# Hybrid decoder block on one core: three sums of w_down's quarters made by adding transfers in DRAM, and MLP activations kept as float32 sums

## The chip, the cores and the metric

The kernel runs on one core of one Trainium2 chip, as one launch. The metric is the device time in microseconds. Engines: TensorE (PE, with PEld for its weight loads), VectorE (DVE), ScalarE (ACT), GpSimd (POOL) and SyncE (SP, which only issues transfers). 16 DMA engines move data for all queues.

## What is computed

One decoder block over 512 tokens of width 1024. Attention has a sparse mixer and a recurrent mixer, merged and projected; then comes a gated MLP of width 2816 with a causal convolution of width 3, and a residual. Only the MLP's end matters here:

```python
def conv_ffn(h, w_up, conv_w, conv_b, w_down):
    u = h @ w_up
    ...
    val, gate = jnp.split(c, 2, axis=-1)          # c: the convolution of u
    return (jax.nn.silu(gate) * val) @ w_down     # (512 x 2816) @ (2816 x 1024)
```

## The kernel before

**Precision.** Every float32 operand of a projection is split into two float32r halves, high and low: ACT copies the high half (`whi`), DVE or POOL subtracts it from the value (`wlo`). A product is then three passes of matmuls: high by high, low by high, high by low.

**Seven products for eight.** The down projection is cut in quarters: the activations in tokens 0 to 255 and 256 to 511, and features 0 to 1407 (left: `l0`, `l1`) and 1408 to 2815 (right: `r0`, `r1`); w_down in the same halves of rows, and halves of columns. Seven products of sums of quarters replace eight products of quarters. They are called by number. The activations' factors are `l0` (1), `s1 = l1 + r1` (5), `s2 = s1 - l0` (6), `s3 = l0 - l1` (7), `s4 = r0 - s2` (3), `r0` (2) and `r1` (4). The weights' factors are the first quarter (1), the difference of two quarters (5), that of three (6), a difference (7), a quarter (3), another (2), and a difference of all four (4). Each product runs over `CH`, six blocks of 256 rows of weights (one of 128). The list `items` has 42 entries, in three groups: for each block products 1, 5, 6; then for each block 7, 3; then 2, 4. In PSUM, products 1 and 2 use the banks `BX` (`ps_a`), 5 and 3 `BY` (`ps_b`), 6, 7 and 4 `BZ` (`ps_mm`). At the end of product 6 and of product 5 DVE adds earlier results (`ev`, kept by ACT) into a bank, and products 7 and 3 go on in it.

**Who prepares.** In the MLP, `sums` makes for each pair of feature tiles the four sums on DVE, and splits `l0`, `s1`, `s2`, `s3` at once (`split`, four ACT copies and four DVE subtractions of 128x256). In the down projection, `prepare` runs two items ahead of `product`: it calls `difference` (a subtraction of weights on DVE: the sums for 5, 6, 7 and 4), splits the weights (`parts`) and, for products 3 and 4, the activations (`operand`). `spare_half` splits the right half's `r0` into the place of `l0` two items after each item of product 1. `load_next` issues the loads of w_down on SP into six places, each when its last user is prepared. Here PE, DVE and ACT run in the order of the program.

**Attention.** PE's order is the program's; a loop over twelve `units` makes scores, transposes and values, and puts matmuls of two projections between them (`filler`). From 298 us these are the eight tiles of w_proj_b, each eight matmuls with `whi` and then four with `wlo`. The subtraction for `wlo` of these eight tiles is made by POOL (line 307), in its queue among its transfers.

Of the kernel before, what the change touches and what calls it, by code (L numbers as in the profile page):

```python
# [12 lines left out]
F32 = mybir.dt.float32  # L13
F32R = mybir.dt.float32r
# [69 lines left out]
def hybrid_block(ctx: ExitStack, tc: tile.TileContext, A: dict, out: bass.AP):  # L84
# [203 lines left out]
    urgent = []  # L288

    def wsplit_():  # L290
        if loads:
# [1023 lines left out]
    nfill = [5, 5, 6, 6, 7, 8, 10, 10, 10, 9, 9, 6]  # L1315
    with tc.manual_schedule(engines=KTS):
# [4 lines left out]
        for i, u in enumerate(units):  # L1321
            if u not in quarters:
                turns(u)
# [136 lines left out]
    tmp = hB[:, 256 * NFH:256 * (NFH + 3)].rearrange("p (k n) -> p k n", k=3)  # L1460
    split = [fp.tile([128, 2, NFH, 256], F32R, name=f"s{j}", tag=f"s{j}") for j in range(4)]
# [20 lines left out]
    w_down = A["w_down"][0]  # L1482
# [8 lines left out]
    for js, last, froms in (((1, 5, 6), (1, 6, 5), ((1, 0, 0), (5, 0, 1), (6, 1, 1))),  # L1491
                            ((7, 3), (7, 3), ((7, 0, 1), (3, 1, 1))), ((2, 4), (2, 4), ((2, 1, 0),))):
        for c, n in CH:
            items += [(j, c, n) for j in (last if c + n == NFH else js)]
            at = {q[0]: k for k, q in enumerate(items) if q[1] == c}
            last_of = {1: (1, 5), 5: (5, 6), 6: (0, 6), 7: (7, 7), 3: (3, 7), 2: (2, 4)}
            fetch += [(*f, c, n, tuple(at[q] if q else 0 for q in last_of[f[0]])) for f in froms]

    raws, turns3, turn, place, start, users = {}, itertools.count(), places(), [], [], [(-1, -1)] * 6

    def load_next():
# [3 lines left out]
        i = place[0]  # L1505
        if not fetch or len(ready) <= users[i][0] or len(summed) <= users[i][1] or (i > 3 and not T2):
            return False
        j, kh, fh, c, n, users[i] = fetch.pop(0)
# [6 lines left out]
        r0 = 128 * (NFH * kh + c)  # L1515
        nc.sync.dma_start(raw, w_down[r0:r0 + 128 * n, 512 * fh:512 * fh + 512].rearrange("(k p) n -> p k n", p=128))
        raws[j, c] = raw
        return True

    def parts(x, n):  # L1520
# [3 lines left out]
        else:  # L1524
            hi, lo = (dn.tile([128, 1024 + p_], F32R, name=k, tag=k)[:, 0:512 * n].rearrange("p (k n) -> p k n", k=n)
# [5 lines left out]
    summed = []  # L1531
# [20 lines left out]
    T1 = set()  # L1552
# [7 lines left out]

    def operand(j, c, n):
# [9 lines left out]
    ready, T2, Sb, X1 = [], [], [], []  # L1571

    def prepare():
        k = len(ready)
        j, c, n = items[k]
        while len(summed) < min(k + 2, len(items)):
            difference()
        ready.append((parts(summed[k], n), operand(j, c, n)))
# [6 lines left out]
    for n_, f in enumerate(order):  # L1585
# [9 lines left out]
        if n_ % 2 == 0:  # L1595
            tt(cv, cv, cg, ALU.mult)
            left = cv
# [4 lines left out]
    dn_cm, dn = pool("down", "right")  # L1602
    T2.append(dn.tile([128, NFH, 512], F32, name="T2"))
# [4 lines left out]
    def add_out(t, hf, x, cs=slice(0, 512), queue=None):  # L1608
        o = X1[0][:, hf, t, cs]
        tt(o, o, x, ALU.add)  # L1610
# [102 lines left out]
```

## Time and profile before

| | us |
|---|---|
| median of three runs (813.38 to 814.07) | 813.43 |
| profiled execution | 813.09 |
| its span | 811.4 |
| PE busy | 801.7 |
| DVE busy | 589.8 |
| ACT busy | 428.8 |
| POOL busy | 66.1 |

The span is what the profiler saw of one execution; 1.7 us of its time lie around it. A busy time counts the time in which an engine has an instruction in work. PE's matmuls overlap, so the pace is read from the distance of starts. Issuing a transfer is not counted as busy, save on POOL, where the row of an issue is its time on that engine. The MLP's up projection runs from about 450 to 701 us, the down projection from 701 to 807.

### The profile page before, as it was taken

The page shows a single profiled execution, that of the slowest core. Times are in us where ns is not written, and L with a number is a line of the kernel's source. Part 1 is how long each engine was busy: PE and PEld are TensorE (multiplying, and loading weights), DVE is VectorE, ACT ScalarE, POOL GpSimd, SP SyncE. Part 2 cuts the span into 40 slices and gives each one's busy share as a digit, 9 for nine tenths or more (in the row PEclk, how much of TensorE's full clock was granted, in tenths as well). Part 3 has the DMA queues.
Part 4 walks back from the last instruction along what each step waited for, and adds up shares of the span by engine and source line. Part 5 has one row for each costly group of instructions (what it writes and reads, how often), then busy time and mean ns, then how long its engine had stood idle before and what let it go on. Part 6 is the DMA issues. An engine that isn't in the chain of part 4 may idle for free.

```text
span 811.4 us, 13524 instructions
## 1 busy us (share of the span) xinstructions
PE 801.7 (99%) x5253; PEld 654.7 (81%) x5253; DVE 589.8 (73%) x1139; ACT 428.8 (53%) x851; POOL 66.1 (8%) x98
## 2 busy tenths in 40 slices
PE   8999999999999999999999999999999999999997
PEld 7777788987777887787888988888888888887886
DVE  6478879983656678889665576677667666898895
ACT  6766654553545668778344454444444444446452
POOL 6100011031000152111000000000000000000010
PEclk9999999999999999999999999999999999999999
DMA  8422223237471331000268133332333233467721
GB/s 242 111 78 76 78 70 87 70 97 216 114 131 53 92 81 28 27 27 27 67 228 277 66 91 92 105 104 84 99 103 102 82 104 104 127 224 231 261 92 52
DMA packets 114124, 89.26 MB, mean 110 GB/s; under 512 B 4629, under 2 KB 98764, under 8 KB 113804
## 3 DMA queue, kind: packets, MB, share of 16 engines
q1 hardware_dynamic: 110416, 82.31, 34.3%
q0 software_dynamic: 2592, 3.61, 1.7%
q10 hardware_dynamic: 1052, 2.48, 1.0%
q8 instruction: 41, 0.67, 0.3%
q14 instruction: 23, 0.19, 0.1%
HBM read 82.35 MB, written 4.39 MB: 107 GB/s over the span
## 4 chain that ended last, share of the span: by engine, by line
PE 94%; DVE 3%; ACT 1%; DMA 1%; issue 1%; POOL 0%; DVEq 0%; POOLq 0%; ACTq 0%
PE ps_mm L123 72%; PE ps_a L123 7%; PE ps_b L123 4%; PE ps_mm L126 3%; PE ps_b L126 2%; PE ps_a L126 2%; PE ps_b L1288 1%; DMA pra<-in_rwkv_ln_b_dram 1%; PE ps_mm L1288 1%; DVE P L1214 0%; POOL pra L170 0%; DVE P L136 0%; ACT P L129 0%; ACT whi L129 0%; PE ps_b L575 0%
## 5 line engine op out<-in xcount | busy, mean ns | idle before, releaser
L123 PE MATMUL ps_mm<-hh,whi 128*128 128x512 f32 (+1 forms) x624 | 242.5, 391 | 0.3 <-DVE hl L141 0.3
L123 PE MATMUL ps_mm<-hl,whi 128*128 128x512 f32 (+1 forms) x624 | 240.3, 387 | 0.0
L129 ACT ACTIVATE whi<-raw 128x1024 fp32r<-128x1024 f32 (+3 forms) x118 | 116.3, 987 | 118.3 <-PE ps_mm L123 87.2
L307 DVE TENSOR_TENSOR wlo<-raw,whi 128x1024 fp32r<-128x1024 f32 (+1 forms) x89 | 104.4, 1174 | 90.1 <-PE ps_mm L123 69.4
L123 PE MATMUL ps_mm<-hh,wlo 128*128 128x512 f32 (+1 forms) x624 | 152.1, 384 | 0.0
L123 PEld LDWEIGHTS ps_mm<-hh,whi 128*128 128x128 f32 x624 | 117.2, 188 | 27.0 <-issue 1.3
L123 PEld LDWEIGHTS ps_mm<-hl,whi 128*128 128x128 f32 x624 | 117.3, 188 | 23.0 <-issue 1.0
L123 PEld LDWEIGHTS ps_mm<-hh,wlo 128*128 128x128 f32 x624 | 115.1, 188 | 23.5
L141 DVE SCALAR_TENSOR_TENSOR hA<-ps_mm,cw,hA 128x511 f32<-128x511 f32 (+1 forms) x88 | 65.4, 746 | 1.5
L129 ACT ACTIVATE hA<-ps_mm,cw 128x512 f32<-128x512 f32 x44 | 34.2, 781 | 19.9 <-PE ps_mm L123 18.3
L129 ACT ACTIVATE P<-P,nm 128x512 f32<-128x512 f32 (+3 forms) x64 | 35.4, 554 | 11.3 <-DVE nm L1214 10.9
L1612 POOL DMA_DIRECT2D out_dram<-XP x6 | 3.3, 546 | 422.3 <-DMA raw<-in_w_down_dram 396.3
L129 ACT ACTIVATE hA<-hA 128x512 f32<-128x512 f32 x22 | 13.9, 633 | 43.6 <-DVE hA L141 43.6
L307 POOL TENSOR_TENSOR wlo<-raw,whi 128x512 fp32r<-128x512 f32 (+3 forms) x13 | 20.9, 1605 | 176.8 <-PE ps_mm L123 142.5
L1214 DVE CUSTOM_DVE_ANT_0 P<-ps_a,AB 128x512 f32<-128x512 f32 (+3 forms) x64 | 29.3, 484 | 1.8 <-PE ps_a L123 1.5
L129 ACT ACTIVATE QK<-ps_mm 128x64 f32<-128x64 f32 (+5 forms) x56 | 14.9, 308 | 18.0 <-PE ps_mm L123 17.9
L132 DVE TENSOR_TENSOR wlo<-raw,whi 128x1024 fp32r<-128x1024 f32 (+1 forms) x16 | 18.5, 1155 | 5.5 <-ACT whi L129 5.5
L123 PE MATMUL ps_mm<-whi,hh 128*128 128x280 f32 (+2 forms) x72 | 22.4, 331 | 0.0
L123 PE MATMUL ps_mm<-whi,hl 128*128 128x280 f32 (+2 forms) x72 | 21.8, 323 | 0.0
L123 PE MATMUL ps_mm<-obT,whi 128*128 128x512 f32 x64 | 20.7, 399 | 0.0
L129 ACT ACTIVATE whi<-T 128x1024 fp32r<-128x1024 f32 (+1 forms) x12 | 11.9, 991 | 16.4 <-DVE T L132 7.5
L129 ACT ACTIVATE whi<-hA 128x1024 fp32r<-128x1024 f32 (+1 forms) x14 | 13.4, 969 | 12.8 <-PE ps_mm L126 3.7
(436 smaller groups left out, 1507.4 us busy)
## 6 DMA issues: line engine op xcount, KB each, us to landing
raw<-in_w_up_dram SPq DMA_DIRECT2D x44, 512.0 KB, 3.7
raw<-in_w_in_dram SPq DMA_DIRECT2D x38, 512.0 KB, 3.8
raw<-in_w_down_dram SPq DMA_DIRECT2D x18, 512.0 KB, 4.1
hA<-in_w_down_dram SPq DMA_DIRECT2D x12, 512.0 KB, 4.6
raw<-in_w_out_dram SPq DMA_DIRECT2D x8, 512.0 KB, 3.6
xt<-in_x_dram SPq DMA_DIRECT2D x4, 512.0 KB, 4.6
raw<-in_cmp_w_v_dram SPq DMA_DIRECT2D x4, 512.0 KB, 3.6
raw<-in_w_proj_b_dram SPq DMA_DIRECT2D x8, 256.0 KB, 2.6
```

What stands on the lines that cost most here:

```text
L123: te.matmul(o, lhsT=l, rhs=r, start=start, stop=stop)
L126: te.matmul(o, lhsT=l, rhs=r, start=False, stop=stop, skip_group_check=True)
L129: sc.activation(o, i, f, **kw)
L132: v.tensor_tensor(o, a, b, op=op)
L141: v.scalar_tensor_tensor(o, a, s, b, op0=op0, op1=op1)
L307: low = eng.tensor_tensor(lo, raw, hi.bitcast(F32), op=ALU.subtract)
L1214: maxima.append(v.tensor_tensor_reduce(out=P[:, i], in0=o, in1=BT[:, h, 384 - 128 * qt:512], scale=-1.0, scalar=-NEG, op0=ALU.add, op1=ALU ...
L1288: te.transpose(pt[:, 128 * i:128 * i + 128], P[:, 4 * x + i, 128 * k:128 * k + 128], ident)
L1612: queue.dma_start(out[0][128 * t:128 * t + 128, 512 * hf + cs.start:512 * hf + cs.stop], o)
```

## The change

Three tensors in DRAM, `T1`, `T2`, `T3` (1408 x 512 each), receive sums of quarters of w_down. POOL issues six transfers from DRAM to DRAM in attention: three copies at unit 1, two that add to what is there at unit 7, and one at unit 11. The signs of the activations are chosen so that the weights are only added: `T1` is the sum of two quarters, `T3` of two others, `T2` of three. Product 4's sum (`T2` plus a quarter) is still made on DVE. Each of the 42 items now has a load of its own.

In the MLP, `sums` makes four float32 sums and splits nothing. In the down projection `operand` splits the activations of products 1, 5, 6, 7 and 3 into three buffers in turn (`Sb`), and `spare_half` splits both parts of the right half for products 2 and 4 (`pre`). Two stores of the output move from POOL's queue to SP's.

```diff
+    w_down = A["w_down"][0]
+    WD = [[w_down[DFF // 2 * i:DFF // 2 * (i + 1), 512 * j:512 * j + 512] for j in range(2)] for i in range(2)]
+    T1, T2, T3 = (dp.tile([DFF // 2, 512], F32, name=f"td{j}") for j in range(3))
+
+    def moved(o, x, **kw):
+        d = nc.gpsimd.dma_start(o, x, max_dma_last_dim=1024, **kw)
+        after(d, on_pool[0])
+        on_pool[:] = [d]
+
+    def weight_sums(i):
+        if i == 1:
+            moved(T1, WD[0][0])
+            moved(T3, WD[0][1])
+            moved(T2, WD[1][1])
+        elif i == 7:
+            moved(T1, WD[0][1], accum_op=ALU.add)
+            moved(T3, WD[1][1], accum_op=ALU.add)
+        elif i == 11:
+            moved(T2, T1, accum_op=ALU.add)
...
         for i, u in enumerate(units):
+            weight_sums(i)
...
-    def sums(i, lf, rt):
-        l0, l1, r0, r1 = lf[:, 0:256], lf[:, 256:512], rt[:, 0:256], rt[:, 256:512]
-        s1, s2, s3 = (tmp[:, j] for j in range(3))
-        tt(s3, l0, l1, ALU.subtract)
-        tt(s1, l1, r1, ALU.add)
-        tt(s2, s1, l0, ALU.subtract)
-        tt(s4[:, i], r0, s2, ALU.subtract)
-        for w, x in zip(split, (l0, s1, s2, s3)):
-            act(w[:, 0, i], x)
-            tt(w[:, 1, i], x, w[:, 0, i].bitcast(F32), ALU.subtract)
+    def sums(i, l1, rt):
+        tt(s3[:, i], a1[:, i], l1, ALU.subtract)
+        tt(s1[:, i], rt[:, 256:512], l1, ALU.subtract)
+        tt(s2[:, i], s1[:, i], a1[:, i], ALU.add)
+        tt(s4[:, i], s2[:, i], rt[:, 0:256], ALU.subtract)
...
+    source = {1: WD[0][0], 5: T1, 6: T2, 7: T3, 3: WD[1][1], 2: WD[1][0], 4: T2}
...
+        nc.sync.dma_start(raw, source[j][128 * c:128 * (c + n)].rearrange("(k p) n -> p k n", p=128))
...
     def difference():
-        j, c, n = items[len(summed)]
-        x = raws.get((j, c))
-        if j == 1 and items[len(summed) + 1][0] == 6 or j == 5 and (5, c) not in T1:
-            T1.add((5, c))
-            y = raws[5, c]
-            tt(y, y, raws[1, c], ALU.subtract)
-        if j == 6:
-            t = T2[0][:, c:c + n]
-            tt(t, x, raws[5, c], ALU.subtract)
-            x = t
-        elif j == 7:
-            tt(x, raws[3, c], x, ALU.subtract)
-        elif j == 4:
-            t = T2[0][:, c:c + n]
-            tt(t, raws[2, c], t, ALU.subtract)
-            x = t
-        summed.append(x)
+        k = summed[0]
+        if items[k][0] == 4:
+            tt(raws[k], raws[k], raws[k - 1], ALU.add)
+        summed[0] += 1
...
     def operand(j, c, n):
-        if j in (1, 5, 6, 7):
-            w = split[(1, 5, 6, 7).index(j)]
-            return w[:, 0, c:c + n], w[:, 1, c:c + n]
-        if j == 2:
-            return split[0][:, 0, c:c + n], split[0][:, 1, c:c + n]
-        x = s4[:, c:c + n] if j == 3 else right[:, c:c + n, 256:512]
-        i = next(turnsb) % 5
-        return halves_of(*(Sb[0][:, i, q, 0:256 * n].rearrange("p (k n) -> p k n", k=n) for q in range(2)), x)
+        if j in (2, 4):
+            return pre[0][:, j // 4, 0, c:c + n], pre[0][:, j // 4, 1, c:c + n]
+        x = {1: a1, 5: s1, 6: s2, 7: s3, 3: s4}[j][:, c:c + n]
+        i = next(turnsb) % 3
+        return halves_of(*(Sb[:, i, q, 0:256 * n].rearrange("p (k n) -> p k n", k=n) for q in range(2)), x)
...
     def spare_half(c, n):
-        halves_of(split[0][:, 0, c:c + n], split[0][:, 1, c:c + n], right[:, c:c + n, 0:256])
+        for q in range(2):
+            halves_of(pre[0][:, q, 0, c:c + n], pre[0][:, q, 1, c:c + n], right[:, c:c + n, 256 * q:256 * q + 256])
...
-                if j == 1:
+                if j == 1 and c < CH[-1][0]:
                     spare_half(c, n)
+                elif j == 3 and c == CH[0][0]:
+                    spare_half(*CH[-1])
```

On POOL the transfers of attention stand among the splits of w_proj_b (`wlo`); `td_3314`, `td_3316` and `td_3315` are `T1`, `T3` and `T2`. Before:

```order
L1105 DMA sq<-kc 32x64 x6
L307 TENSOR_TENSOR wlo<-raw,whi 128x512
L1103 DMA Vr<-vt 32x256 x16
L1105 DMA sq<-kc 32x64 x2
L307 TENSOR_TENSOR wlo<-raw,whi 128x512 x7
L1612 DMA out_dram<-XP 128x512 x6
```

And in the changed kernel:

```order
L1105 DMA Vr<-vt 32x256 x16
L1107 DMA sq<-kc 32x64 x2
L307 TENSOR_TENSOR wlo<-raw,whi 128x512
L1324 DMA td_3314<-in_w_down_dram 1408x2x256
L1324 DMA td_3316<-in_w_down_dram 1408x2x256
L1324 DMA td_3315<-in_w_down_dram 1408x2x256
L307 TENSOR_TENSOR wlo<-raw,whi 128x512 x3
L1324 DMA td_3314<-in_w_down_dram 1408x2x256
L1324 DMA td_3316<-in_w_down_dram 1408x2x256
L307 TENSOR_TENSOR wlo<-raw,whi 128x512 x3
L1324 DMA td_3315<-td_3314 2816x256
L1617 DMA out_dram<-XP 128x512 x4
```

Three issues stand ahead of the third tile's split, two ahead of the sixth's, one behind the last.

On DVE, where product 6 and then product 5 end (the additions into `ps_mm` and `ps_b`), `hA<-hA` and `raw<-hA,raw` being subtractions of weights and `s_5187` the place of the spare half. Before:

```order
L132 TENSOR_TENSOR wlo<-raw,whi 128x1024
L132 TENSOR_TENSOR ps_mm<-ps_mm,hA 128x512 x2
L132 TENSOR_TENSOR hA<-hA 128x1024
L132 TENSOR_TENSOR wlo<-hA,whi 128x1024
L132 TENSOR_TENSOR Sb<-hB,Sb 128x512
L132 TENSOR_TENSOR s_5187<-right,s_5187 128x512
L132 TENSOR_TENSOR ps_b<-ps_b,hA 128x512 x2
```

And in the changed kernel:

```order
L132 TENSOR_TENSOR wlo<-raw,whi 128x1024
L132 TENSOR_TENSOR Sb<-s_5198,Sb 128x512
L132 TENSOR_TENSOR ps_mm<-hA,ps_mm 128x512 x2
L132 TENSOR_TENSOR wlo<-hA,whi 128x1024
L132 TENSOR_TENSOR Sb<-hB,Sb 128x512
L132 TENSOR_TENSOR ps_b<-ps_b,hA 128x512 x2
```

Between the two additions two operations are gone, a subtraction of weights and the spare half's split.

On DVE at the MLP's end, from the last convolution on (line 141), with the splits of the second and third product's weights (`wlo`, `wlo_6833` and `wlo_6763`). Before:

```order
L132 TENSOR_TENSOR T_6812<-raw 128x1024
L141 SCALAR_TENSOR_TENSOR hA<-ps_mm,cw,hA 128x511
L132 TENSOR_TENSOR wlo<-raw,whi 128x1024
L141 SCALAR_TENSOR_TENSOR hA<-ps_mm,cw,hA 128x510
L132 TENSOR_TENSOR wlo_6833<-T_6812,whi_6832 128x1024
L132 TENSOR_TENSOR right<-hA 128x512
L132 TENSOR_TENSOR raw<-raw,hA 128x1024
```

And in the changed kernel, where the second product's weight split is the operation ahead of the first row:

```order
L141 SCALAR_TENSOR_TENSOR hA<-ps_mm,cw,hA 128x511
L132 TENSOR_TENSOR Sb<-a1s_5196,Sb 128x512
L141 SCALAR_TENSOR_TENSOR hA<-ps_mm,cw,hA 128x510
L132 TENSOR_TENSOR wlo_6763<-raw,whi_6762 128x1024
L132 TENSOR_TENSOR right<-hA 128x512
L132 TENSOR_TENSOR Sb<-s_5197,Sb 128x512
L132 TENSOR_TENSOR a1s_5196<-right,hA 128x256
```

The weight subtractions (`T_6812`, `raw<-raw,hA`) are gone, and splits of activations (`Sb`) stand between.

## Rows read from the trace of the kernel before

**Rows 1.** The page's busy time, share of the span and instructions by engine

```profile
PE 801.7 (99%) x5253; PEld 654.7 (81%) x5253; DVE 589.8 (73%) x1139; ACT 428.8 (53%) x851; POOL 66.1 (8%) x98
```

**Rows 2.** Waits of PE, whole span: us in total, times, longest

```profile
PE ps_b L126 <- DVE ps_b L132: 0.7, 1, 0.7
```

**Rows 3.** Stretches: length; busy PE, PEld, DVE, ACT, POOL; clock; DMA share; GB/s

```profile
0.00:50.00 50.00, 46.49 (x221) 36.68 (x221) 31.93 (x72) 32.24 (x48) 17.36 (x31) 1.00 0.57 164
350.00:400.00 50.00, 49.21 (x575) 38.97 (x575) 39.93 (x154) 32.62 (x108) 4.32 (x4) 1.00 0.13 39
...
740.00:750.00 10.00, 9.35 (x42) 7.43 (x40) 8.54 (x12) 7.39 (x11) 0.00 (x0) 1.00 0.69 227
800.00:811.40 11.40, 6.92 (x37) 5.78 (x35) 5.68 (x9) 1.49 (x2) 1.08 (x2) 0.94 0.25 93
```

**Rows 4.** Chain that ended last, down projection: start, us, engine, line, count

```profile
709.08 2.72 PE ps_a L123 x12
711.80 2.96 PE ps_b L123 x12
```

**Rows 5.** Timeline of ACT and DVE, product 5's end: start, us, what, idle before

```profile
745.25 1.05 ACT L129 ACTIVATE whi<-hA 128x1024 fp32r<-128x1024 f32 x1
746.34 1.23 DVE L132 TENSOR_TENSOR wlo<-hA,whi 128x1024 fp32r<-128x1024 f32 x1 [0.55 <-ACT whi L129]
...
748.08 0.68 DVE L132 TENSOR_TENSOR s<-right,s 128x512 fp32r<-128x512 f32 x1
748.68 1.29 DVE L132 TENSOR_TENSOR ps_b<-ps_b,hA 128x512 f32<-128x512 f32 x2
```

**Rows 6.** Timeline of DVE and PE at the MLP's end

```profile
700.96 1.23 DVE L132 TENSOR_TENSOR T<-raw 128x1024 f32<-128x1024 f32 x1 [2.52 <-PE ps_mm L123]
...
702.10 0.74 DVE L141 SCALAR_TENSOR_TENSOR hA<-ps_mm,cw,hA 128x511 f32<-128x511 f32 x1
...
702.76 1.22 DVE L132 TENSOR_TENSOR wlo<-raw,whi 128x1024 fp32r<-128x1024 f32 x1
...
706.20 1.07 PE L123 MATMUL ps_mm<-whi,s 128*128 128x512 f32 x4
```

**Rows 7.** Timeline of POOL in attention: splits of w_proj_b's tiles 2, 5, 8

```profile
308.79 1.30 POOL L307 TENSOR_TENSOR wlo<-raw,whi 128x512 fp32r<-128x512 f32 x1
...
349.15 1.28 POOL L307 TENSOR_TENSOR wlo<-raw,whi 128x512 fp32r<-128x512 f32 x1 [6.93 <-ACT whi L129]
...
378.81 1.30 POOL L307 TENSOR_TENSOR wlo<-raw,whi 128x512 fp32r<-128x512 f32 x1 [7.12 <-ACT P L129]
```

**Rows 8.** Timeline of PE: first use of `wlo` of tiles 3 and 6

```profile
347.23 0.40 PE L123 MATMUL ps_mm<-obT,wlo 128*128 128x512 f32 x1
...
377.11 0.85 PE L123 MATMUL ps_mm<-obT,wlo 128*128 128x512 f32 x3
```

**Rows 9.** POOL's operations by shape: count, busy us, mean ns, idle before

```profile
L1103 POOL DMA_DIRECT2D Vr<-vt x16 | 8.2, 518 | 0.0
...
L1612 POOL DMA_DIRECT2D out_dram<-XP x6 | 3.3, 546 | 422.3 <-DMA raw<-in_w_down_dram 396.3 <-DVE XP L132 26.0
```

**Rows 10.** The stretch in which POOL issues the sixteen Vr transfers, columns as rows 3

```profile
300.00:310.00 10.00, 9.94 (x52) 8.35 (x52) 9.20 (x31) 7.74 (x19) 9.98 (x19) 1.00 0.29 82
```

**Rows 11.** The page's DMA queues (q1 SP, q0 POOL): packets, MB, engines' share

```profile
q1 hardware_dynamic: 110416, 82.31, 34.3%
q0 software_dynamic: 2592, 3.61, 1.7%
```

**Rows 12.** Output projection: a stretch, columns as rows 3, and timeline rows

```profile
424.00:428.00 4.00, 4.00 (x19) 3.34 (x18) 2.36 (x2) 0.89 (x1) 0.00 (x0) 1.00 0.95 365
...
417.02 0.41 ACTq L1378 DMA_DIRECT2D x<-in_x_dram  x1
...
428.78 0.69 DVE L132 TENSOR_TENSOR x<-x,ps_mm 128x512 f32<-128x512 f32 x1 [1.72 <-DMA x<-in_x_dram]
...
435.33 0.39 PE L123 MATMUL ps_mm<-Wh,mTh 128*128 128x512 f32 x1
```

More of the change, by code (lines that the diff above doesn't have):

```diff
@@ L286, in wsplit @@
             wsplit_()
-    urgent = []
+    urgent, on_pool = [], []
     def wsplit_():
@@ L307, in wsplit_ @@
             low = eng.tensor_tensor(lo, raw, hi.bitcast(F32), op=ALU.subtract)
+            if eng is nc.gpsimd:
+                on_pool[:] = [low]
             if behind:
@@ L1459, in hybrid_block @@
     s4 = hB[:, 0:256 * NFH].rearrange("p (k n) -> p k n", k=NFH)
-    tmp = hB[:, 256 * NFH:256 * (NFH + 3)].rearrange("p (k n) -> p k n", k=3)
-    split = [fp.tile([128, 2, NFH, 256], F32R, name=f"s{j}", tag=f"s{j}") for j in range(4)]
+    a1s1 = fp.tile([128, 2, NFH, 256], F32, name="a1s1", tag="a1s1")
+    a1, s1 = a1s1[:, 0], a1s1[:, 1]
+    s2, s3 = (fp.tile([128, NFH, 256], F32, name=f"s{j}") for j in (2, 3))
     right = fp.tile([128, NFH, 512], F32, name="right", tag="right")
@@ L1490, in hybrid_block @@
     items, fetch = [], []
-    for js, last, froms in (((1, 5, 6), (1, 6, 5), ((1, 0, 0), (5, 0, 1), (6, 1, 1))),
-                            ((7, 3), (7, 3), ((7, 0, 1), (3, 1, 1))), ((2, 4), (2, 4), ((2, 1, 0),))):
+    source = {1: WD[0][0], 5: T1, 6: T2, 7: T3, 3: WD[1][1], 2: WD[1][0], 4: T2}
+    for js, last in (((1, 5, 6), (1, 6, 5)), ((7, 3), (7, 3)), ((2, 4), (2, 4))):
         for c, n in CH:
+            first = len(items)
             items += [(j, c, n) for j in (last if c + n == NFH else js)]
[L1495 to L1499, printed above, removed]
+            fetch += [first + 1 if j == 2 else k for k, (j, _, _) in list(enumerate(items))[first:]]
+    raws, turns3, turn, place, start, users = [], itertools.count(), places(), [], [], [-1] * 6
     def load_next():
@@ L1504, in load_next @@
             place.append(next(turn))
-        i = place[0]
-        if not fetch or len(ready) <= users[i][0] or len(summed) <= users[i][1] or (i > 3 and not T2):
-            return False
-        j, kh, fh, c, n, users[i] = fetch.pop(0)
+        i, k = place[0], len(raws)
+        if k == len(items) or len(ready) <= users[i] or (i > 3 and not dn):
+            return False
+        users[i] = fetch[k]
+        j, c, n = items[k]
         place[0] = next(turn)
@@ L1514, in load_next @@
             raw = hA[:, o:o + 512 * n].rearrange("p (k n) -> p k n", k=n)
-        r0 = 128 * (NFH * kh + c)
-        nc.sync.dma_start(raw, w_down[r0:r0 + 128 * n, 512 * fh:512 * fh + 512].rearrange("(k p) n -> p k n", p=128))
-        raws[j, c] = raw
+        nc.sync.dma_start(raw, source[j][128 * c:128 * (c + n)].rearrange("(k p) n -> p k n", p=128))
+        raws.append(raw)
         return True
@@ L1575, in prepare @@
         j, c, n = items[k]
[L1576 removed]
+        while summed[0] < min(k + 2, len(items)):
             difference()
[L1578 removed]
+        ready.append((parts(raws[k], n), operand(j, c, n)))
     def spare_half(c, n):
[L1581 removed]
+        for q in range(2):
+            halves_of(pre[0][:, q, 0, c:c + n], pre[0][:, q, 1, c:c + n], right[:, c:c + n, 256 * q:256 * q + 256])
     spent.append(load_next)
@@ L1595, in hybrid_block @@
         if n_ % 2 == 0:
-            tt(cv, cv, cg, ALU.mult)
-            left = cv
+            tt(a1[:, f], cv[:, 0:256], cg[:, 0:256], ALU.mult)
+            left = cv[:, 256:512]
+            tt(left, left, cg[:, 256:512], ALU.mult)
         else:
@@ L1601, in hybrid_block @@
     close(h2_cm)
-    dn_cm, dn = pool("down", "right")
-    T2.append(dn.tile([128, NFH, 512], F32, name="T2"))
+    dn_cm, dnp = pool("down", "right")
+    dn.append(dnp)
+    pre.append(dnp.tile([128, 2, 2, NFH, 256], F32R, name="pre"))
     BX, BY, BZ = [pa(), pa()], [pb(), pb()], [mmb(), mmb()]
@@ L1658, in product @@
             for i in range(2):
-                add_out(i, 0, b[i], queue=nc.gpsimd)
+                add_out(i, 0, b[i], queue=nc.sync)
         else:
```

16 lines of the change are left out of this document (7 added, 9 removed).

## Prediction

> **What bounds the kernel now.** I read the engines' busy times first. TensorE (PE) is busy 801.7 of 811.4 us, DVE 73%, ACT 53%, POOL 8% [rows 1], so only 9.6 us of the span are PE's idle time. Then the stretches with such idle time [rows 3]: 3.5 us lie in the first 50 us, before the projections run, and 4.5 us in the last 11.4 us, behind the last product; the change touches neither end. Of the 1.6 us left, 0.65 us lie between 740 and 750 us, in the down projection, and 0.8 between 350 and 400 us, in attention. The waits of PE say what the 0.65 us are: one wait of 0.7 us for an addition into a PSUM bank on DVE [rows 2]. Last, the chain of work through the down projection: a product of twelve matmuls takes 2.72 us, and one takes 2.96 [rows 4]; the 0.24 us are the other place where PE runs late there. So what DVE and ACT do is hidden under PE almost everywhere, and the change, which leaves the number and the order of PE's products as they are, has about 0.9 us to win.
>
> **Part 1: sums of weights leave DVE.** Before, 24 subtractions of weights (four for each of the six blocks of rows) run on DVE in the down projection, the large ones 1.22 to 1.23 us each. The change keeps six (the additions for product 4) and makes the others in DRAM. Against that, the halves of the activations that were made in the MLP are now made in the down projection: per block of two rows of tiles, one ACT copy and one DVE subtraction for each of products 1, 5, 6 and 7, and a second pair beside product 1 for the right half. Per block of the first group DVE then does 3 splits of weights and 5 of activations, by the distance of starts 3 x 1.14 + 5 x 0.60 = 6.4 us, against 5 x 1.14 + 0.60 = 6.3 before, under 8.16 us of PE (3 x 2.72). In the second group it goes from 4.0 to 3.5 us under 5.44, in the third from 4.0 to 3.4. All of it stays covered; in the MLP the removed splits were covered too (PE has no wait there), and their removal is worth nothing.
>
> Where it matters is the order at two places. **At the change from product 5 to product 3** PE waits 0.66 us for the addition into `ps_b` that starts at 748.68. DVE comes to it over the split at 746.34 (which waits for ACT's `whi` of 745.25, and that ends at 746.30), a split `Sb` of 0.60 and a split `s` for the spare half, 748.08 to 748.68 [rows 5]. In the new order the spare half's split and the weight subtraction ahead are gone. The subtraction hides behind ACT's `whi` and gives nothing; the spare half gives 0.60 us. The addition then starts at about 748.08, and 0.06 us of the wait are left: **-0.60 us**. What is late next is ACT's `whi`, unchanged.
>
> **At the MLP's end** DVE has two convolution steps and the right half's product to do while PE runs the first three products. Starts there are 1.14 us apart after a large split and 0.66 after a convolution step [rows 6]. The weight split of the second product can start at 700.96, when the last up-projection matmul frees its buffer. In the new order, from there: split, convolution, `Sb`, convolution, split, product, `Sb`: 700.96 + 1.14 + 0.66 + 0.60 + 0.66 + 1.14 + 0.60 = 705.76, so the third product's low half is there at 706.44. PE begins that product at 706.20 and uses the low half one matmul (0.23 us) later. That is no slack at all: I take **+0.2 us**, with bounds of 0 and 1 us (two further splits of DVE in front). The 0.24 us lost at 711.80 before should go, because the weight subtraction ahead of that product goes: **-0.24**.
>
> **Part 2: the loads.** 42 loads of w_down instead of 36; the six new ones stand in the last group, where two loads of 512 KB now feed 5.44 us of PE and six places are free in turn. The first loads from the new sums come about 680 us, some 240 us after the sums. No cost. Two more stores of the output go from POOL's queue to SP's; the end is set by the last additions behind them, no cost.
>
> **Part 3: six transfers on POOL.** Each moves 1408 x 512 floats, 2.88 MB in 2816 pieces of 1 KB. They stand in POOL's order among the splits of w_proj_b, which PE waits for. Three plain ones follow the split at 308.79, so they start at 310.1. The next split was made at 327, but PE uses its `wlo` first at 347.23; made in 1.30 us, it may start as late as 345.9. POOL has **35.8 us for three, 11.9 each** [rows 7, 8]. The two sums stand behind the split of 349.15; the next one's `wlo` is used at 377.11, so they have **25.4 us, 12.7 each**. The last sum stands behind the split of 378.81, with nothing behind it on POOL until the output's stores at 776. What POOL spends on such an issue no row shows. The nearest rows: 518 ns for 32 pieces (Vr), 546 for 128 (the output) [rows 9]. By their slope (28 ns for 96 pieces) 2816 pieces cost 1.3 us; in proportion to 128 pieces, 12.0 us; if POOL were held until the data has moved, more (below). I take 1.3, since the rows hardly rise with size: three copies 4 us, two sums 2.7, **no cost**. An issue in proportion would miss by 0.2 us.
>
> POOL's rows also bear on DVE's port: sixteen Vr issues in a row took 518 ns each while DVE was busy 9.20 of 10 us [rows 9, 10], no more than the others. The Trainium skill (SBUF — State Buffer, section "SBUF: two separate sides") says that DVE operations in a two-port mode lock GpSimd out of writing descriptors, and gives 620 ns becoming 3100. These rows don't show it; by that factor of five the issue would be an estimated 6.7 us, still under 11.9 and without cost, and from the proportional price it would be 60 us, which belongs to rival A.
>
> How long the data takes: POOL's queue moved 3.61 MB in 2592 packets at 1.7% of 16 engines' span, 85 ns per packet; SP's 110416 packets took 34.3%, 40 ns per 745 bytes, 296 GB/s [rows 11]. So a copy takes 9.7 us (SP's rate) to 15.0 us (176 packets per engine at 85 ns); a sum, which reads twice, up to twice that, 19 to 30. Copies end at 339 to 355, the first two sums at 389 to 415, the third at 409 to 445. Nobody waits for them; they only share the engines.
>
> **The sum.** The profiled execution took 813.09 (span 811.4): 813.09 - 0.60 - 0.24 + 0.2 = 812.45. The median of the runs is 0.34 above the profiled one, so the forecast for the median is **812.8**, 0.6 us under 813.43. A measurement of this kernel can tell 0.2%, 1.6 us, from no change; this is within it. Its own range is 811.9 to 814.5.
>
> **Rival A, slower: POOL is held.** If POOL stays with a transfer until its data has moved, or writes its pieces far more slowly than the small issues suggest, the splits behind come late and PE waits for `wlo`. With 9.7 us per copy and 19.4 per sum, the copies fit (29 of 35.8) and the sums miss by 13.4 us (38.8 against 25.4): 826. With 15 and 30 the misses are 9.2 and 34.6: 856. It decides from 11.9 us per copy or 12.7 per sum. Against it: the flat prices in [rows 9]. 10%.
>
> **Rival B, slower: the third sum meets the output projection.** There the 16 engines are nearly full (0.95 from 424 to 428 us). The residual x, issued at 417.02, lands for DVE at 428.78; the bank that this addition frees is taken by PE at 435.33, so it may slip by 5.9 us (435.33 - 429.47) [rows 12]. If the sum still runs then and takes half the engines, x takes twice its 11.7 us and PE waits up to 5.8 us: 818.3. It decides when the third sum ends after about 417; my bounds are 409 and 445. That the sharing is by turns is what the Trainium skill says (DMA: Bandwidth & Descriptors, "Issuing engines are not separate DMA queues": DMAs of all issuers run on the same 16 engines and interleave); no row here has two large streams of which one is POOL's. 12%.
>
> **Rival C, slower: the MLP's end** runs late by more than 1.8 us because DVE never catches up from the chain above: 814.5 to 816. Against it: DVE gains 1.8 us per block on PE. 3%.
>
> **Rival D, faster by more than 1.6 us.** It needs all idle time that the change can reach, or matmuls closer than 2.72 us per twelve. The trace has that pace everywhere, with DVE full or not. 3%.
>
> **How the numbers follow.** Forecast 72%, A 10%, B 12%, C 3%, D 3%: faster 0.03, same 0.72, slower 0.25. The range takes the forecast's own and B: 811.7 to 818.7, 84%.
>
> **What would show it.** In the changed profile PE should have no wait above 0.3 us for `ps_b` in the down projection, POOL's six issues should last under 3 us each, and its splits should start at the times they had. A POOL issue over 12 us, or a wait of PE for `wlo` between 345 and 390 us, shows A; a late x with a PE wait at 435 us shows B; PE waits between 703 and 715 us show C. A changed pace of matmuls would make the whole reading wrong.

## The result and the profile after

The changed kernel took **824.38 us** (median of four runs, 822.34 to 828.53) against 813.72 for the kernel before beside it: a ratio of 1.0139, with a 95% interval of 1.012 to 1.0158. Forecast were 812.8 us and a range of 811.7 to 818.7, so the prediction was wrong. The profiled execution took 824.33 us with a span of 822.6, 11.2 us more than before.

The page's busy time by engine, which answers [rows 1]:

```profile
PE 805.4 (98%) x5253; PEld 656.7 (80%) x5253; DVE 576.4 (70%) x1112; ACT 427.8 (52%) x831; POOL 84.9 (10%) x102
```

The longest waits of PE (us in total, times, longest), which answer [rows 2]:

```profile
PE ps_a L123 <- DVE nm L1216: 4.9, 3, 2.7
PE ps_b L123 <- issue: 2.7, 1, 2.7
PE ps_mm L351 <- DVE h L136: 1.5, 2, 1.3
...
PE ps_mm L351 <- DVE rx_m L138: 1.2, 1, 1.2
PE ps_b L126 <- DVE ps_b L132: 0.7, 1, 0.7
```

DVE and ACT have less to do, as meant, and PE has the same 5253 matmuls, but new waits. Stretches of the span say where (columns as in [rows 3]):

```profile
310.00:320.00 10.00, 8.60 (x64) 6.49 (x63) 7.89 (x22) 8.17 (x20) 8.95 (x4) 1.00 0.64 197
350.00:360.00 10.00, 9.20 (x57) 7.21 (x57) 9.37 (x30) 7.43 (x23) 8.48 (x3) 1.00 0.23 42
360.00:370.00 10.00, 7.00 (x47) 4.94 (x46) 8.86 (x26) 5.29 (x17) 4.19 (x2) 0.98 1.22 190
370.00:380.00 10.00, 10.00 (x62) 8.26 (x61) 8.30 (x35) 7.75 (x26) 1.22 (x1) 0.85 1.22 202
390.00:400.00 10.00, 6.85 (x217) 5.21 (x213) 4.00 (x12) 2.35 (x8) 0.69 (x1) 1.00 1.21 206
400.00:410.00 10.00, 9.93 (x125) 8.34 (x126) 4.72 (x11) 3.20 (x8) 0.00 (x0) 0.83 1.14 204
```

Start by start of PE's matmuls, after lies behind before by 1.3 us more around 315, 1.6 us more from 355 to 365, 4.4 us more by 374, 2.4 us more by 400 and 1.2 us more by 407. That is 10.9 us, all in attention. In two stretches the granted clock is 0.85 and 0.83 in the mean, so for a part of them at the lower of its two levels (1.2 GHz); each lies behind an idle time of PE of 2.67 us. Outside attention there are 1.05 us in the first 17 us of the span (the waits at L351, before anything that the change touches; in the first experiment below, with the same code there, `rx_m` is 0.2), 0.13 us in the down projection, and 0.9 us won behind the last product: 10.9 + 1.05 + 0.13 - 0.9 = 11.2.

**What PE waits for.** Three of the five losses lead through one line of DVE, the scaling of attention's weights by a factor per partition (L136, `scale`). The timeline of POOL gives the issues of the six transfers, that of DVE the scalings:

```profile
310.92 8.02 POOL L1324 DMA_DIRECT2D td<-in_w_down_dram  x3
...
352.74 10.16 POOL L1324 DMA_DIRECT2D td<-in_w_down_dram  x2
...
388.42 2.27 POOL L1324 DMA_DIRECT2D td<-td  x1
```

```profile
312.05 1.76 DVE L136 TENSOR_SCALAR P<-P,sm 128x512 f32<-128x512 f32 x1
315.85 1.00 DVE L136 TENSOR_SCALAR P<-P,sm 128x512 f32<-128x512 f32 x2
318.75 1.28 DVE L136 TENSOR_SCALAR P<-P,sm 128x512 f32<-128x512 f32 x3
...
353.71 1.92 DVE L136 TENSOR_SCALAR P<-P,sm 128x384 f32<-128x384 f32 x1
357.48 0.58 DVE L136 TENSOR_SCALAR mx<-mx 128x8 f32<-128x8 f32 x1
359.27 3.82 DVE L136 TENSOR_SCALAR P<-P,sm 128x384 f32<-128x384 f32 x2
```

The same instructions in the kernel before:

```profile
310.94 0.48 DVE L136 TENSOR_SCALAR P<-P,sm 128x512 f32<-128x512 f32 x1
...
351.35 0.41 DVE L136 TENSOR_SCALAR P<-P,sm 128x384 f32<-128x384 f32 x1
...
353.84 0.17 DVE L136 TENSOR_SCALAR mx<-mx 128x8 f32<-128x8 f32 x1
...
355.52 0.75 DVE L136 TENSOR_SCALAR P<-P,sm 128x384 f32<-128x384 f32 x2
```

After, those that meet an issue take 1.76 in place of 0.48, 1.92 in place of 0.41, 0.58 in place of 0.17, and 3.82 (1.46 and 2.44) in place of 0.75; the two at 315.85, which meet the last 0.4 us of an issue, take 1.00 in place of 0.88. Other forms of DVE (tensor_tensor, copies from PSUM, reductions) keep their durations beside the issues. The ends of the held scalings follow POOL's rows: the first copy's issue ends at 313.58 and the scaling at 313.81, the second copy's at 316.23 and the scaling at 316.46. The packets of the copies run from 314.3 on, so the first hold was over before data moved. The rows of the two sums overlap: the first runs from 352.74 to 357.83, the second is

```profile
355.41 7.49 POOL L1324 DMA_DIRECT2D td<-in_w_down_dram  x1
```

The scalings end at 355.63, 358.06 and 363.08, about 0.2 us behind the second row's start, the first one's end and the second one's end. Behind a late scaling DVE's next maxima (`nm`) come late, and PE waits for these.

One part of the longest wait, 2.67 us at 369.21, has another source. On the chain that leads to it stands a pair of tensor_tensor on four numbers per partition:

```profile
365.80 0.87 DVE L132 TENSOR_TENSOR sm<-sm,gts 128x4 f32<-128x4 f32 x2
```

Before, the pair took 0.24 us (358.99). After, it meets POOL's own subtraction for `wlo` (365.29 to 366.58), and its first is through at 366.60. So 0.63 us of this wait come from POOL's arithmetic, which the late scalings had moved beside it, and not from an issue.

**The stall at 397 us** is another thing. The chain of waits (start, us, what) has it as time in which PE waited for nothing that the profile shows:

```profile
395.06 1.79 PE ps_mm L123 x8
...
397.40 2.67 issue
```

It stands between two of some two hundred short matmuls (32x64) at attention's end. In the kernel before, PE stopped at the same matmul (389.26) for 0.25 us. The table behind the experiment without the last sum says what PE lacked.

**The down projection** has the wait for `ps_b` (0.66 us) as before. The chain of waits through it, to be read beside [rows 5]:

```profile
755.58 0.54 issue
756.12 0.70 DVE ps_mm L132
756.90 0.64 ACT hA L129 x2
757.99 1.06 ACT whi L129
759.11 1.11 issue
760.82 0.70 DVE ps_b L132
761.57 3.02 PE ps_b L126 x12
```

### The profile page after: what moved, and what is told of

Same layout as the page of the kernel before. It is cut to its first block, busy times and chain, and to the rows that moved or that the text cites. A ratio compares the mean times of both kernels' runs of the same rounds, so it can differ in the third digit from the quotient of the medians.

```text
span 822.6 us, 13515 instructions
## 1 busy us (share of the span) xinstructions
PE 805.4 (98%) x5253; PEld 656.7 (80%) x5253; DVE 576.4 (70%) x1112; ACT 427.8 (52%) x831; POOL 84.9 (10%) x102
## 4 chain that ended last, share of the span: by engine, by line
PE 91%; DVE 4%; ACT 2%; DMA 1%; issue 1%; SPq 0%; DVEq 0%; ACTq 0%
PE ps_mm L123 71%; PE ps_a L123 7%; PE ps_b L123 4%; PE ps_mm L126 3%; PE ps_b L126 2%; PE ps_a L126 2%; DVE P L136 1%; DMA raw<-in_w_in_dram 1%; DVE P L1216 1%; ACT P L129 1%; PE ps_b L1290 1%; PE ps_mm L1290 0%; ACT whi L129 0%; DVE PTs L1156 0%; PE ps_b L577 0%
## 5 line engine op out<-in xcount | busy, mean ns | idle before, releaser
L129 ACT ACTIVATE whi<-raw 128x1024 fp32r<-128x1024 f32 (+3 forms) x125 | 124.2, 995 | 143.5 <-PE ps_mm L123 114.3
L307 DVE TENSOR_TENSOR wlo<-raw,whi 128x1024 fp32r<-128x1024 f32 (+1 forms) x89 | 104.6, 1176 | 115.7 <-PE ps_mm L123 93.9
L132 DVE TENSOR_TENSOR wlo<-raw,whi 128x1024 fp32r<-128x1024 f32 (+1 forms) x23 | 27.6, 1199 | 11.7 <-ACT whi L129 7.4
L129 ACT ACTIVATE whi<-hA 128x1024 fp32r<-128x1024 f32 (+1 forms) x19 | 17.6, 927 | 20.5 <-PE ps_mm L126 6.4
L132 DVE TENSOR_TENSOR wlo<-hA,whi 128x1024 fp32r<-128x1024 f32 (+1 forms) x19 | 20.0, 1055 | 11.2 <-ACT whi L129 11.1
L123 PE MATMUL ps_a<-KH,qst 128*128 128x512 f32 (+2 forms) x48 | 18.7, 393 | 5.0 <-DVE nm L1216 4.9
```

What stands on the lines that cost most here:

```text
L123: te.matmul(o, lhsT=l, rhs=r, start=start, stop=stop)
L129: sc.activation(o, i, f, **kw)
L132: v.tensor_tensor(o, a, b, op=op)
```

## Experiments

The theories are these: **1**, POOL's issue of a transfer of many pieces holds DVE's scaling; **2**, the transfers' packets on the 16 engines delay something that PE needs at 397 us; rivals: the new work in the down projection, or data traffic as such, or that any place costs the same. In the diffs, `-` is the changed kernel unless the text says otherwise, and `...` marks a cut.

**Without the transfers.**

```diff
-            weight_sums(i)
...
-    source = {1: WD[0][0], 5: T1, 6: T2, 7: T3, 3: WD[1][1], 2: WD[1][0], 4: T2}
+    source = {1: WD[0][0], 5: WD[0][1], 6: WD[1][1], 7: WD[0][1], 3: WD[1][1], 2: WD[1][0], 4: WD[0][0]}
```

> The six transfers are left out; products 5, 6, 7 and 4 read quarters of w_down in place of the sums (so the output is another one), with the same loads, splits and matmuls. Theory 1 (POOL's issue of the transfers holds DVE's scaling of the attention weights, 7.3 of the 11.2 us) and theory 2 (the sums' traffic makes PE's next instructions late at 397 us, 3.6 us with the clock behind it) both put the whole loss on the transfers: 812 to 814 us, all PE waits over 1 us between 300 and 410 us gone. Rival 3 (the new splits in the down projection or other moved work costs): above 816 us, with the attention's waits gone but the time not back.

Measured: 813.49 us, ratio to before 1.0007 (0.9998 to 1.0016). The whole loss belongs to the transfers; everything else in the change is worth nothing that can be measured. The rival of the down projection falls.

**The issue without the data.** All pieces are there, but each moves 16 bytes; the products' sources are those of the experiment above.

```diff
...
-        d = nc.gpsimd.dma_start(o, x, max_dma_last_dim=1024, **kw)
+        d = nc.gpsimd.dma_start(o, x[:, 0:8], max_dma_last_dim=16, **kw)
...
```

> The issue by itself: the same six transfers with the same number of pieces (2816), from POOL at the same places, but each piece of 16 bytes, so that 45 KB move in place of 2.88 MB; products use quarters of w_down as in e1_no_transfers (the output is another one). Theory 1: the issue is as long as before (2.7 and 5.1 us) and DVE's scaling is held as before: waits of PE at 312 and 353 to 370 us, some 7 us with the clock, 819 to 821 us. Theory 2: without traffic no stall at 390 us. If the hold came from the data's traffic: as e1_no_transfers, 813.5 us.

Measured: 825.51 us, ratio 1.0141 (1.0121 to 1.0162). Timeline of POOL, then of DVE:

```profile
310.43 8.02 POOL L1324 DMA_DIRECT2D td<-in_w_down_dram  x3
352.24 10.17 POOL L1324 DMA_DIRECT2D td<-in_w_down_dram  x2
...
311.56 1.76 DVE L136 TENSOR_SCALAR P<-P,sm 128x512 f32<-128x512 f32 x1
...
353.21 1.92 DVE L136 TENSOR_SCALAR P<-P,sm 128x384 f32<-128x384 f32 x1
...
358.77 3.82 DVE L136 TENSOR_SCALAR P<-P,sm 128x384 f32<-128x384 f32 x2
```

Issues and holds are the same to 0.01 us with 1/64 of the bytes: the hold belongs to the issue. But theory 2 missed: the stall at the same matmul is 2.96 us, and the time 4.5 us above the upper end of what I expected. A stretch says why bytes were the wrong measure:

```profile
390.00:400.00 10.00, 7.19 (x211) 5.47 (x210) 3.79 (x12) 2.10 (x6) 0.28 (x1) 1.00 0.76 21
```

At 21 GB/s the DMA engines are still busy for 0.76 of the time: small pieces occupy them too. Theory 2 has to be about their time, not about bytes.

**Another form of the scaling.** The transfers stay.

```diff
+            elif units.index(u) in (1, 7, 8):
+                tt(P[:, i], P[:, i], sm[:, i:i + 1].to_broadcast([128, 128 * (qt + 1)]), ALU.mult)
             else:
                 ts(P[:, i], P[:, i], sm[:, i:i + 1], None)
```

> The transfers stay; only the three units of attention whose scaling meets a transfer's issue (units 1, 7 and 8) scale by a tensor_tensor with the factor broadcast instead of a tensor_scalar with a factor per partition; same values. Theory 1, if the hold is one of that instruction's form: the rows of 1.76, 1.92 and 3.82 us become some 0.6 us each, PE's waits at 312 to 314 and 353 to 370 us go with the clock loss behind them, 817 to 819 us; the stall at 397 us stays (theory 2). If the transfers' traffic or the issue as such holds DVE whatever the form: the new rows are as long, 823 to 825 us.

Measured: 820.52 us, ratio 1.0092 (1.0078 to 1.0106), 3.9 us under the changed kernel and 1.5 us above the upper end of what I expected. Timeline of DVE in the two places:

```profile
311.27 0.69 DVE L132 TENSOR_TENSOR P<-P,sm 128x512 f32<-128x512 f32 x1
...
352.72 0.55 DVE L132 TENSOR_TENSOR P<-P,sm 128x384 f32<-128x384 f32 x1
...
355.21 1.85 DVE L136 TENSOR_SCALAR mx<-mx 128x8 f32<-128x8 f32 x1
...
358.28 1.02 DVE L132 TENSOR_TENSOR P<-P,sm 128x384 f32<-128x384 f32 x2
```

The new form runs through the issues unheld. The hold now finds the next instruction of the old form: a tensor_scalar on eight numbers per partition, 0.17 us before, takes 1.85. So it goes by form, not by size. This and a scaling of unit 2 at 317.20 cost PE 0.80 and 0.83 us. The new form has a price of its own, 0.69 us in place of 0.48, and PE has a wait of 0.63 us for `nm` at 367.78, behind four of them, that neither the kernel before nor the changed one has.

**Longer pieces**: 2 KB, so 1408 of them per transfer.

```diff
-        d = nc.gpsimd.dma_start(o, x, max_dma_last_dim=1024, **kw)
+        d = nc.gpsimd.dma_start(o, x, max_dma_last_dim=2048, **kw)
```

> As the changed kernel, but in pieces of 2 KB instead of 1 KB (1408 per transfer). Theory 1: if POOL's issue goes by the piece, it falls from 2.67 to 1.3 us per copy and from 5.08 to 2.5 per sum, the longest hold of DVE from 3.8 to under 2 us, and the time by 2 to 5 us: 819 to 822. If the issue goes by bytes: no change, 824. The stall at 397 us stays in both (theory 2), unless sums in longer pieces are through earlier.

Measured: 816.8 us, ratio 1.0041 (1.0026 to 1.0057), 2.2 us under the lower end of what I expected. Timeline of POOL:

```profile
311.29 2.63 POOL L1324 DMA_DIRECT2D td<-in_w_down_dram  x3
352.26 3.08 POOL L1324 DMA_DIRECT2D td<-in_w_down_dram  x2
```

An issue takes 0.9 us per copy and 1.5 per sum, a third of before for half the pieces, and the two sums are issued by 355.3, with one scaling held, by 0.56 us (one beside the copies is held by 0.42). PE's waits for `nm` are down from 4.9 to 0.5 us in all. The stall remains, with 2.38 us.

**Plain copies from ACT** instead of POOL, six of them, to separate tiles.

```diff
-        d = nc.gpsimd.dma_start(o, x, max_dma_last_dim=1024, **kw)
-        after(d, on_pool[0])
+        d = sc.dma_start(o, x, max_dma_last_dim=1024)
+        after(d, on_act[0])
...
-            moved(T1, WD[0][1], accum_op=ALU.add)
+            moved(U1, WD[0][1])
```

> All six transfers become plain copies of the same size (no adding; the last three go to tiles that nobody reads, so products 5, 6 and 7 and 4 use unsummed weights and the output is another one), issued by ACT at about the same places, and POOL issues none of them. Theory 1: DVE's scaling keeps its 0.48 us at all places and PE has no wait at 312 or 353 to 361 us. Theory 2: the stall of PE at about 390 us can stay if a copy runs then, up to 3.6 us. Together 812.5 to 817 us. If traffic within DRAM were the cause of DVE's long rows, they would stay: 819 to 824 us.

Measured: 836.19 us, ratio 1.0282 (1.0267 to 1.0296): outside both expectations. Timeline of ACT:

```profile
314.96 0.68 ACTq L1326 DMA_DIRECT2D td<-in_w_down_dram  x1
...
315.68 15.16 ACTq L1326 DMA_DIRECT2D td<-in_w_down_dram  x2
```

The first copy is issued in 0.68 us; the next two keep ACT for 15.16 us, and PE waits 9.3 us for a transpose's copy. PE has no wait for `nm` over 0.5 us, as theory 1 wants, and the stall is 3.45 us with plain copies running. The next two issues, from 371.03 on, keep ACT for another 6.7 us, and PE waits 3.9 us behind them at 387.5. DVE's scalings beside the copies keep 0.48 us. As a cure the queue is no better.

**Without the last sum**, on the kernel with the other form.

```diff
         elif i == 11:
-            moved(T2, T1, accum_op=ALU.add)
+            pass
```

> The kernel of e2_other_form without the last sum (T2 += T1), so that products 6 and 4 use other weights and the output is another one. Theory 2 (PE's next instructions come late because a transfer within DRAM fills the 16 engines at 392 us): the first two sums alone are through by about 390 us, so the stall of 2.65 us among the small matmuls goes, and with it the clock loss of 1.5 us behind it: 816 to 817.5 us. If the stall comes from the new place of the code or from anything that the transfers don't do: it stays, 820 us.

Measured: 818.26 us, ratio 1.0061 (1.0046 to 1.0075); 0.8 us above the upper end of what I expected. The stall falls from 2.65 to 1.28 us and doesn't go: the first two sums fill the engines until about 392 us, and PE comes to the place at 392. It shrinks, but this alone doesn't prove theory 2.

**What PE lacks at the stall.** The page of every run lists a queue with 41 instruction packets. That of the changed kernel (packets, MB, engines' share):

```profile
q8 instruction: 41, 0.67, 0.3%
```

The page doesn't say whose instructions these are. But in all thirteen traces each of the 41 packets, of 16 KB, starts with PE at the same one of its 5253 matmuls, 30 of them within 10 matmuls and all within 62. The 25th packet is the one before the stall. By the traces' records of packets and matmuls, in us:

| kernel | PE, 128 matmuls ahead | packet starts | packet ends | matmul starts | PE stopped for |
|---|---|---|---|---|---|
| before | 385.68 | 386.63 | 387.81 | 389.26 | 0.25 |
| without the transfers | 386.39 | 387.28 | 388.37 | 389.65 | 0.00 |
| changed | 394.07 | 397.63 | 398.60 | 400.07 | 2.67 |
| small pieces | 393.65 | 398.26 | 399.86 | 400.94 | 2.96 |
| other form | 388.99 | 392.75 | 393.70 | 394.98 | 2.65 |
| long pieces | 387.58 | 391.01 | 391.98 | 393.29 | 2.38 |
| copies from ACT | 404.64 | 409.07 | 410.12 | 411.44 | 3.45 |
| without the last sum | 388.91 | 391.20 | 392.15 | 393.52 | 1.28 |

In all thirteen kernels the matmul starts 1.1 to 1.5 us behind this packet's end. Where no transfer within DRAM runs, the packet starts 0.8 to 1.1 us behind the matmul of the second column; where one runs, 2.3 to 4.6, and PE stops for roughly the difference. Without the last sum the two other sums' packets end at 392.05, and the packet, started at 391.20, is less late. So theory 2 holds: the transfers make PE's next instructions late, and even the kernel before has no slack at this place. That the packet waits its turn on the DMA engines is argued from their share (1.21 here, 0.19 before), not seen packet by packet.

**In the MLP.** The same six transfers as a block behind the second pair of up-projection columns.

```diff
-            weight_sums(i)
...
+            if n_ == 1:
+                on_pool[:] = [nc.gpsimd.tensor_tensor(mark, right[:, 0, 0:8], right[:, 0, 8:16], op=ALU.add)]
+                for i in (1, 7, 11):
+                    weight_sums(i)
```

> The same six transfers with their sums, from POOL, but behind the second pair of up-projection columns in the MLP (about 500 us) instead of in attention; a small POOL addition that reads the MLP's result sets the place. Theory 1: DVE has no tensor_scalar there, so nothing is held and the attention is as before. Theory 2: the sums' packets (some 90 us of them) can make PE's instructions late there too: 2.5 us per late block and the clock behind it. So 812 to 814 us by theory 1 alone, 815 to 820 with one or two stalls of PE in the MLP by theory 2. Rival 3 (the place doesn't matter, the transfers cost the same anywhere): 822 to 825 us.

Measured: 841.53 us, ratio 1.0352 (1.0338 to 1.0366), worse than anywhere else and 16.5 us above the highest of the three expectations. The attention is as before; the loss is in PE's largest wait:

```profile
PE ps_mm L123 <- ACT whi L129: 20.8, 9, 8.4
```

Whose it is, the issues of loads from 510 to 600 us say (count, size, median us to landing):

```profile
raw<-in_w_up_dram SPq DMA_DIRECT2D x12, 512.0 KB, 20.5
```

A load of w_up, 3.7 us from issue to landing in the kernel before, takes 20.5, and ACT's `whi` waits for it. Both my theories gave the place less than it cost: here the engines' time is the bound, as rival B had it for another place.

**In slices**, the same bytes spread over the MLP.

```diff
...
+        if pieces:
+            on_pool[:] = [nc.gpsimd.tensor_tensor(mark, here[:, 0:8], here[:, 8:16], op=ALU.add)]
+            for _ in range(min(4, len(pieces))):
+                o, x, r, kw = pieces.pop(0)
+                moved(o, x, r, **kw)
```

> The six transfers with their sums, cut into 66 slices of 256 KB (128 rows) and issued four at a time behind each pair of up-projection products (17 places, one each 11.4 us), so that a load of w_up never stands beside more than a few of them. Theory 1: nothing of DVE is held, the attention is as before. If the loss in e4_in_mlp (28.7 us between 510 and 563 us) is the loads' share of the engines (68 GB/s granted, 92 needed), the slices leave room: by bytes 1 MB of slices takes some 5 us of each 11.4, and the two loads 2 x 1.8; 812 to 814.5 us. If each slice still pushes a load past its time, PE waits for whi again: 818 to 835 us.

Measured: 813.83 us, ratio 1.0006 (0.9997 to 1.0014). 27.7 us of the block's cost are gone. PE has no wait in the MLP.

**The same, with the small tile elsewhere** (`-` is the kernel with slices).

```diff
-    mark = fp.tile([128, 8], F32, name="mark")
...
+    mark = fp.tile([128, 64], F32, name="mark")
```

> e6_slices, with the one small tile that it adds (32 bytes per partition, ahead of the operands of the down projection) made 256 bytes and put behind them. In e6_slices and e4_in_mlp the products of the down projection ran 2.80 us per twelve matmuls, in all others 2.72. If that comes from where the operands lie: 2.72 again and 1.4 us less, about 812.4 us. If it comes from the transfers in the MLP: 2.80 stays, 813.8.

Measured: 812.51 us, ratio 0.9992 (0.9984 to 1.0001), 1.3 us less. A timeline row of PE in the kernel with slices, four matmuls of the down projection:

```profile
712.71 1.10 PE L123 MATMUL ps_b<-whi,Sb 128*128 128x512 f32 x4
```

The same four here:

```profile
711.95 1.07 PE L123 MATMUL ps_b<-whi,Sb 128*128 128x512 f32 x4
```

With the 32 bytes in front, the matmuls of products 1, 5, 6, 7 and 3 were 3% slower, 2.80 us in place of 2.72 per twelve. Those of products 2 and 4, which read their activations from another tile (`pre`), had 2.72 in the kernel with slices too, so it goes with where the operands lie and not with the transfers.

**Own banks for product 3**, on top of it.

```diff
...
-    pbank = {1: BX, 2: BX, 5: BY, 3: BY, 6: BZ, 7: BZ, 4: BZ}
+    pbank = {1: BX, 2: BX, 5: BY, 3: BW, 6: BZ, 7: BZ, 4: BZ}
...
+            if items[k][0] == 3 and items[k][1] == CH[3][0]:
+                for i in range(2):
+                    add_out(i, 1, BY[i])
```

> e10_slices_aligned, and product 3 adds into two PSUM banks of its own instead of the banks of product 5; the sum that PE waited for (0.66 us at the change from product 5 to product 3) is then taken by DVE later, by two more additions of 0.7 us. If my step for that place had the right wait and only the wrong cause of its end: no wait over 0.3 us in the down projection, 0.6 us less than e10_slices_aligned, about 811.8 us. If DVE's or ACT's splits end last there anyway, the wait turns up at whi or wlo: as e10_slices_aligned.

Measured: **811.84 us, ratio 0.9982 (0.9973 to 0.9991)**: the wait is gone, and this version beats both kernels, the one before by 0.18%. That is less than the 0.2% that the prediction takes as the limit of one such measurement, but it is the only version here whose interval lies under 1.

**In attention, but harmless.** It has the other form, pieces of 2 KB, and the last sum in 11 slices in the MLP.

```diff
...
-        d = nc.gpsimd.dma_start(o, x, max_dma_last_dim=1024, **kw)
+        d = nc.gpsimd.dma_start(o, x, max_dma_last_dim=2048, **kw)
...
+            r = pieces.pop(0)
+            moved(T2[128 * r:128 * r + 128], T1[128 * r:128 * r + 128], accum_op=ALU.add)
```

> The attention's place made harmless by both theories: three copies and two sums stay in attention, in pieces of 2 KB, the three units that meet them scale by tensor_tensor, and the last sum is cut into 11 slices of 128 rows in the MLP. Theory 1: no hold, PE has no wait over 0.5 us for DVE between 305 and 375 us. Theory 2: the two sums are through at about 383 us, before PE's burst of small matmuls at 389, so no stall there. Together 812.5 to 814.5 us. If one of the two is wrong its loss stays: 815 to 818.

Measured: 813.9 us, ratio 1.001 (1.0001 to 1.0019). The two sums' packets end at 385.5, before the 25th instruction packet (388.28), and the stall is back at 0.2 us. What PE still waits for of `nm`:

```profile
PE ps_a L123 <- DVE nm L1216: 1.2, 3, 0.6
```

The longest, 0.63, is again the one behind the new form. Both causes together are the loss, and each goes with what makes it.

## Why the prediction was wrong

**The step that failed: "three copies 4 us, two sums 2.7, no cost".** I priced the issues for what stands behind them on POOL. There the answer was right though the price was not: 2.67 us per copy, 5.08 per sum and 2.27 for the last, in place of 1.3 (proportional to 128 pieces it would have been 12.0), still within the 11.9 and 12.7 that I had worked out. POOL's splits came in time, and rival A did not occur. But POOL's time was the wrong question. While it issues transfers of so many pieces, DVE's tensor_scalar from SBUF to SBUF isn't done, and by way of `nm` PE waits: 7.3 of the 10.9 us lost in attention, with the clock, lie behind such waits (0.63 of them by POOL's subtraction). I did weigh the port, in one direction only: whether a busy DVE slows POOL, from 518 ns per issue in [rows 9, 10]. Whether POOL slows DVE, I never asked. The trace before has two answers:

```profile
306.43 1.27 DVE L136 TENSOR_SCALAR P<-P,sm 128x512 f32<-128x512 f32 x3
...
327.80 1.14 DVE L132 TENSOR_TENSOR sC<-sC,mx 128x256 f32<-128x256 f32 x1
```

Three scalings beside the last Vr issues, of 32 pieces each, kept 0.48 us each, so those small issues gave no warning. But beside POOL's subtraction for `wlo` (327.36 to 328.66) a tensor_tensor took 1.14 in place of its usual 0.42: that POOL holds DVE at all was to be seen, and nothing waited for it there. From how many pieces on an issue holds a scaling, no run here tells.

The Trainium skill (SBUF — State Buffer, section "SBUF: two separate sides") has both directions: the port pair that DVE and GpSimd share is an exclusive lock, and whichever starts first, a DVE operation in a two-port mode or a GpSimd operation, keeps it for its whole instruction. The trace agrees with the direction, and the scaling by tensor_tensor that ran unheld fits that the section names an operation with two SBUF inputs only against a GpSimd operation that reads SBUF; the tensor_tensor at 365.80, held by POOL's subtraction, fits that too. On the length it agrees for the copies, whose holds end with the issue (313.81 behind 313.58). For the sums it differs: the scaling that began at 353.71 was through at 355.63, while POOL's first sum was in issue until 357.83. The rows of the two sums overlap there, and the hold ended 0.22 us behind the second one's start.

**"Nobody waits for them; they only share the engines"** failed too. The times were about right: the last sum landed 21 us after its issue, at about 410, where the bounds were 409 and 445, so the output projection was not met and rival B did not occur. But the engines' time counts for others as well. In attention it was the instructions for PE's short matmuls, 2.4 us and 1.2 by the clock behind them; in the MLP, when I put the block there, it was the loads.

**-0.60 at the change from product 5 to 3 did not come.** The step said: "What is late next is ACT's `whi`, unchanged". It was not unchanged. The spare half's split is gone, but a split of product 7's activations now stands ahead of the addition into `ps_mm`, as in the new order printed ahead of the prediction:

```profile
755.51 0.69 DVE L132 TENSOR_TENSOR Sb<-s,Sb 128x512 fp32r<-128x512 f32 x1
```

That addition starts 0.61 us later against PE than before (756.12 for 743.37, with PE's matmuls there 12.14 later), so ACT's `hA`, its `whi` and the rest of the chain move by the same 0.6. I had followed the chain back to `whi` and stopped one step too early. With banks of its own for product 3 the wait went, for 0.67 us: its size was right, its cause was not.

**-0.24 and +0.2 came** as worked out, by the chain that ended last: the piece at 724.06 takes 2.72, and the third product is 0.25 us late:

```profile
718.37 2.97 PE ps_mm L123 x12
```

The +0.2 was a choice between bounds of 0 and 1 us, so that it came so close is partly luck.

**The loads and stores cost nothing**, as said; the end is even 0.9 us shorter (last transfer's issue to the end of the span: 3.9 before, 2.9 after). That two stores went from POOL to SP fits, but was not tried apart.

**The range.** Its upper end, 818.7, came from rival B alone. The mechanisms that decided had no price in it: the hold of DVE wasn't asked for, and the transfers were taken to cost nobody anything before the output projection.

## What to carry to other kernels

A large transfer issued by POOL had a victim on another engine here. Before placing one beside a busy DVE, count its pieces, look for tensor_scalar on SBUF in the same microseconds, and ask who waits for that; longer pieces, another form of the instruction or another place each helped here. Then ask what else needs the 16 engines' time while it runs, loads and PE's own instructions above all, the latter where many short matmuls use them up; look at the page's instruction queue when PE stops for no wait. Spread large transfers in slices where the loads leave room. When a chain is followed back to see what a removed step gives, follow it past the next engine, to the step that sets that one's start.

## What the runs showed of the hardware

- A tensor_scalar from SBUF to SBUF waited for POOL's issue of a transfer of 1408 or 2816 pieces, up to 2.0 us (2.44 in place of 0.42), even on 128x8 numbers (0.17 to 1.85 us); tensor_tensor, reductions and operations from PSUM did not. Beside issues of 32 pieces it did not wait either (0.48 us).
- A tensor_tensor with both inputs in SBUF waited for POOL's own tensor_tensor (1.14 us in place of 0.42, before and after).
- The issue went by pieces, not by bytes: 8.02 us for three copies with 2.88 MB or with 45 KB each. The first two sums took 5.08 us each where a copy took 2.67, with 2816 pieces of each; with 1408 it was 1.5 and 0.9. The last sum, between two of the new tensors, took 2.27 with 2816.
- PE stood still behind the same matmul in each kernel where a transfer in DRAM ran at that time (1.28 to 3.45 us), and 0.4 us or less where none did. The matmul came 1.1 to 1.5 us behind the end of the same instruction packet in every kernel, and that packet started late by about the stall.
- ACT's queue took one copy of 2816 pieces in 0.68 us and was then kept 15.16 us by two more.
- 32 bytes in front of the matmuls' operands: 2.80 us instead of 2.72 per twelve, in the products whose activations lay behind them. Why, no run here tells.
